# Small steps of a two-layer decoder trunk move between ScalarE, GpSimd and VectorE

## The chip, the cores and the metric

The kernel runs on one core of a Trainium2 chip. The metric is the time of one execution on the device in microseconds (us). The engines are called as the profile calls them: PE (TensorE, matmuls; PEld its weight loads), DVE (VectorE), ACT (ScalarE), POOL (GpSimd) and SP (SyncE, which issues the DMAs).

## The reference

One inference step of a trunk of two layers, for one prompt of 512 rows and 8 sample rows that share the weights (width 1024). Cut to what matters here:

```python
def causal_conv(x, buf, w, b):                 # both layers; 3072 channels, 4 taps
    xp = concatenate([buf, x], axis=1)
    out = b + sum(xp[:, i:i + L] * w[i] for i in range(4))
    return silu(out), xp[:, L:]                # the last 3 rows are an output

# layer 0: gated DeltaNet (8 heads) and GLA (4 heads) beside each other, then one output projection
# GLA, per head and chunk:   o = qe @ S + p @ v;   S = alast * S + kdec.T @ v
# per head:                  o2 = rmsnorm(o2, gla_norm_g) * silu(gate)
# layer 1: SSD, 32 heads in 4 groups; per head and chunk:
#                            y = elam * (c @ h) + m @ xdt;  h = last * h + xdec.T @ b
# per group:                 y = rmsnorm(y * silu(z), ssd_norm_g)
```

A sample has one new row and a state of its own, in the convolution (its last 3 rows, `buf`) as in the recurrences.

## The kernel before

The activations are held transposed, 128 channels on the partitions and 520 columns free: 512 of the prompt, cut in 4 chunks of 128, and 8 of the samples. A projection takes 128 columns of weights: `split_w` (L234) makes of them a rounded part on ACT (`w`, L248) and the rest by a subtraction on DVE, of every third or so on POOL; `project_half` (L258) runs 24 matmuls (L264 to L266, the last reads the rest) into one of two `pj` banks, or in layer 1 also `px`, first for columns 0 to 255, then for 256 to 519, whose last 8 are the samples.

`conv` (L431) takes the two halves: ACT copies them to SBUF (`xr`, L436), ACT scales `xr` by one tap (L437), POOL copies the last 11 columns (3 of the prompt, 8 of the samples) to `tail` (L438), DVE adds three taps, ACT takes the tanh (L442), DVE makes the SiLU of it. There are 48 such calls, 24 in each layer. `conv_samples` (L446) does the samples' convolution later, from `tail`, for 2 or 4 tiles at a time: two POOL operations, a tanh on ACT, one scaled product on DVE.

In layer 0, `gdn_samples` (L738) makes the samples' step of the DeltaNet per head, and `gla_head` (L837) a GLA head: per chunk PE makes `pd`, ACT scales it to `sn` (L892), DVE adds the old state; POOL scales the old state to `sp` (L886), which PE multiplies by the queries (L899); ACT squares the result for the norm (L902). After that come the samples: SP loads their states (L940), PE multiplies (L942), transposes (L955), sums squares over the partitions (L964), and the norm and gate are small operations on POOL and DVE. Beside this POOL runs the 62 steps of the triangular inverse (`sb` and `st` 64xN, from `gdn_blocks`, L618).

In layer 1, `ssd_group` (L1222) does a group of 8 heads: two convolutions for `b_` and `c_`, four for x. DVE makes decay matrices (`dec`), `kq` is a convolution's result, L1318 its transposes, L1345 and L1358 the products over chunks. `sample_x` (L1263) calls `conv_samples` and scales; `sample_state` (L1275) runs per pair of heads two POOL products with the state (`sb<-inv,st`), a sum on DVE, two POOL products for the update (`sb<-inv,smh`), 8 scalings on ACT and an addition on DVE. `sample_norm` (L1202) closes two groups.

A scheduler in the tile framework sets the order of the instructions on each engine, from the program's order, the buffers of each tile name (`BUFS`) and its own estimates of durations. So an edit in one place moves instructions elsewhere too. Each engine then runs its list in order, and waits where an input isn't there.

## Time and profile before

| | |
|---|---|
| median of 3 runs | 1144.23 us (1143.73 to 1147.21) |
| the profiled execution, its own time | 1146.9 us |
| its span, first to last instruction | 1145.1 us |
| granted TensorE clock, mean | 0.976 |
| PE busy | 1056.3 us, 92% |
| DVE busy | 763.1 us, 67% |
| ACT busy | 620.4 us, 54% |
| POOL busy | 576.5 us, 50% |
| DMA | 160 MB, 140 GB/s |

Of the span, layer 0 takes the first 650 us or so, layer 1 the rest. The shares are means over stages that differ: a stage is read by the stretch of the trace in which it lies. Names in the trace are those of the tiles; L141 is the helper for products and sums of two tiles, L144 that for a scaled product, so the tile says which step it is. The clock is given as a share of the full 2.4 GHz.

### The profile page before, as it was taken

The page shows a single profiled execution, that of the slowest core. Times are in us where ns is not written, and L with a number is a line of the kernel's source. Part 1 is how long each engine was busy: PE and PEld are TensorE (multiplying, and loading weights), DVE is VectorE, ACT ScalarE, POOL GpSimd, SP SyncE. Part 2 cuts the span into 40 slices and gives each one's busy share as a digit, 9 for nine tenths or more (in the row PEclk, how much of TensorE's full clock was granted, in tenths as well). Part 3 has the DMA queues.
Part 4 walks back from the last instruction along what each step waited for, and adds up shares of the span by engine and source line. Part 5 has one row for each costly group of instructions (what it writes and reads, how often), then busy time and mean ns, then how long its engine had stood idle before and what let it go on. Part 6 is the DMA issues. An engine that isn't in the chain of part 4 may idle for free.

```text
span 1145.1 us, 23024 instructions
## 1 busy us (share of the span) xinstructions
PE 1056.3 (92%) x8900; PEld 1006.4 (88%) x8900; DVE 763.1 (67%) x1265; ACT 620.4 (54%) x1458; POOL 576.5 (50%) x701
## 2 busy tenths in 40 slices
PE   8999989999999898999889989979988988988997
PEld 7999879899899897898889988869978978988997
DVE  5797354657776645656554468799889689766643
ACT  5566345544444644554333556855855765765452
POOL 4144962204143594226152534685497587468542
PEclk8999999999999999899997999999999999999999
DMA  5324245623544325544842434645755654656632
GB/s 162 90 80 110 68 146 157 190 56 107 166 135 117 114 79 165 180 133 136 246 126 71 131 97 132 190 131 149 218 148 149 187 165 132 208 174 194 185 89 76
DMA packets 241731, 160.00 MB, mean 140 GB/s; under 512 B 21463, under 2 KB 221358, under 8 KB 241606
## 3 DMA queue, kind: packets, MB, share of 16 engines
q1 hardware_dynamic: 241622, 158.53, 47.8%
q8 instruction: 70, 1.15, 0.4%
q14 instruction: 39, 0.32, 0.1%
HBM read 127.05 MB, written 31.84 MB: 139 GB/s over the span
## 4 chain that ended last, share of the span: by engine, by line
PE 40%; POOL 18%; DVE 17%; DMA 13%; issue 5%; ACT 4%; SPq 2%; DVEq 0%; POOLq 0%; ACTq 0%
PE pj L265 9%; PE pj L264 9%; PE pj L266 9%; POOL sb L141 8%; DVE f L144 4%; POOL st L141 3%; DVE w L141 2%; DMA sb<-ud 1%; DMA dec<-ldr 1%; PE px L265 1%; DVE st L141 1%; DVE kq L144 1%; PE px L264 1%; PE px L266 1%; DVE of L141 1%
## 5 line engine op out<-in xcount | busy, mean ns | idle before, releaser
L266 PE MATMUL pj<-ua,w 128*128 128x256 f32 x776 | 224.8, 290 | 5.3 <-DVE w L141 3.9
L264 PE MATMUL pj<-ub,w 128*128 128x264 f32 x768 | 225.6, 294 | 1.5 <-ACT ub L339 0.9
L264 PE MATMUL pj<-ua,w 128*128 128x256 f32 x776 | 224.5, 289 | 2.0 <-ACT vg L472 1.3
L266 PE MATMUL pj<-ub,w 128*128 128x264 f32 x768 | 224.4, 292 | 0.0
L265 PE MATMUL pj<-ub,w 128*128 128x264 f32 x742 | 218.3, 294 | 0.0
L265 PE MATMUL pj<-ua,w 128*128 128x256 f32 x750 | 217.0, 290 | 1.4 <-POOL ua L1028 1.4
L141 DVE TENSOR_TENSOR w<-raw,w 128x1024 fp32r<-128x1024 f32 x102 | 140.8, 1381 | 59.0 <-PE pj L265 30.1
L248 ACT ACTIVATE w<-raw 128x1024 fp32r<-128x1024 f32 x123 | 129.7, 1054 | 49.2 <-PE pj L266 10.6
L266 PEld LDWEIGHTS pj<-ua,w 128*128 128x128 f32 x776 | 149.6, 193 | 7.7 <-DVE w L141 4.3
L264 PEld LDWEIGHTS pj<-ua,w 128*128 128x128 f32 x776 | 149.4, 192 | 3.3 <-ACT vg L472 1.5
L264 PEld LDWEIGHTS pj<-ub,w 128*128 128x128 f32 x768 | 147.4, 192 | 3.1 <-ACT ub L339 1.1
L266 PEld LDWEIGHTS pj<-ub,w 128*128 128x128 f32 x768 | 147.1, 192 | 2.2 <-issue 2.0
L144 DVE SCALAR_TENSOR_TENSOR f<-xr,cvw,f 128x512 f32<-128x512 f32 x144 | 136.5, 948 | 17.5 <-ACT f L437 16.0
L265 PEld LDWEIGHTS pj<-ua,w 128*128 128x128 f32 x750 | 144.5, 193 | 3.7 <-issue 1.8
L265 PEld LDWEIGHTS pj<-ub,w 128*128 128x128 f32 x742 | 142.3, 192 | 2.0 <-issue 1.5
L438 POOL COPY tail<-xr 128x11 f32<-128x11 f32 x48 | 31.9, 666 | 86.7 <-ACT xr L436 70.4
L141 POOL TENSOR_TENSOR w<-raw,w 128x1024 fp32r<-128x1024 f32 x20 | 52.1, 2607 | 39.8 <-PE px L265 13.2
L141 POOL TENSOR_TENSOR sb<-inv,st 128x512 f32<-128x512 f32 x32 | 53.6, 1691 | 15.7 <-DMA inv<-bd 9.2
L442 ACT ACTIVATE f<-f 128x512 f32<-128x512 f32 x48 | 30.2, 628 | 56.8 <-DVE f L144 56.6
L1287 ACT ACTIVATE st<-st,c 128x128 f32<-128x128 f32 x128 | 41.2, 395 | 33.7 <-POOL sb L141 33.7
L436 ACT ACTIVATE xr<-pj 128x256 f32<-128x256 f32 (+1 forms) x72 | 27.4, 380 | 41.1 <-PE pj L266 40.8
L1340 ACT ACTIVATE dec<-dec,c 128x128 f32<-128x128 f32 x128 | 40.3, 390 | 10.3 <-DMA dec<-ldr 8.9
(564 smaller groups left out, 2825.3 us busy)
## 6 DMA issues: line engine op xcount, KB each, us to landing
raw<-in_e_w_in_dram SPq DMA_DIRECT2D x56, 512.0 KB
raw<-in_o_w_in_dram SPq DMA_DIRECT2D x40, 512.0 KB
out_dram<-st SPq DMA_DIRECT2D x32, 512.0 KB
raw<-in_e_w_out_dram SPq DMA_DIRECT2D x32, 256.0 KB
st<-in_state_ssd_dram SPq DMA_DIRECT2D x16, 512.0 KB
dec<-ldr SPq DMA_DIRECT2D x32, 256.0 KB
raw<-in_o_w_out_dram SPq DMA_DIRECT2D x32, 256.0 KB
sb<-vd SPq DMA_DIRECT2D x8, 512.0 KB
```

What stands on the lines that cost most here:

```text
L141: eng.tensor_tensor(out, a, b, op=op)
L144: dve.scalar_tensor_tensor(out, a, s, b, op0=op0, op1=op1)
L248: act.activation(wh, rv, AF.Copy)
L264: pe.matmul(ps, wh, uh[b], start=(k == 0), stop=False)
L265: pe.matmul(ps, wh, ul[b], start=False, stop=False)
L266: i0 = pe.matmul(ps, wl, uh[b], start=False, stop=(k == NK - 1))
L436: act.activation(hsl(xr[:, 3:3 + T], b), halves[b], AF.Copy)
L438: pool.tensor_copy(tail[:, :, j], xr[:, TP:TP + 11])
L442: act.activation(th, a, AF.Tanh)
L1287: act.activation(st[:, b], st[:, b], AF.Copy, scale=sc2[:, 1, pr, b:b + 1])
L1340: act.activation(rb[:, chunk(c)], rb[:, chunk(c)], AF.Relu, scale=-1.0, bias=lamc[:, c, h:h + 1])
```

## The change

Six edits, and new buffer counts (`s2` 3 in place of 2, `sp` 2 in place of 1):

1. `conv`: the last 11 columns go to `tail` by ACT, straight from the second half's PSUM bank (five calls of 48 that have no such bank read `xr`).
2. `conv_samples`: the scaled product on DVE becomes two POOL operations, th*a and +a.
3. `gdn_samples`: the last product and sum of each head go from DVE to POOL.
4. `gla_head`: `sp` is made by ACT with a column scale instead of by POOL.
5. End of `gla_head`: two POOL and two DVE operations per head become three POOL operations over both halves.
6. `sample_norm`: eight scaled products on DVE become two POOL operations.

```diff
@@ -111,7 +111,7 @@
 
     BUFS = {
         ...
-        "st": 2, "sb": 2, "smc": 6, "smp": 4, "sms": 9, "jk": 1, "c5": 4, "c2": 1, "jd": 1, "nss": 1, "nrs": 1, "ors": 3, "smt": 1, "s1": 3, "u1": 2, "s2": 2, "smh": 6, "sp": 1, "row": 2,
+        "st": 2, "sb": 2, "smc": 6, "smp": 4, "sms": 9, "jk": 1, "c5": 4, "c2": 1, "jd": 1, "nss": 1, "nrs": 1, "ors": 3, "smt": 1, "s1": 3, "u1": 2, "s2": 3, "smh": 6, "sp": 2, "row": 2,
     }
     PBUFS = {"pj": 2, "po": 2, "pr": 2, "px": 1, "ps": 1}
     uid = [0]
@@ -435,7 +435,7 @@
         for b in range(2) if halves else ():
             act.activation(hsl(xr[:, 3:3 + T], b), halves[b], AF.Copy)
         act.activation(a, xr[:, 3:3 + TP], AF.Identity, scale=cw[:, 72 + j:73 + j], bias=cw[:, 96 + j:97 + j])
-        pool.tensor_copy(tail[:, :, j], xr[:, TP:TP + 11])
+        act.activation(tail[:, :, j], halves[1][:, 253:264] if halves else xr[:, TP:TP + 11], AF.Copy)
         for i in range(3):
             stt(a, xr[:, i:i + TP], cw[:, i * 24 + j:i * 24 + j + 1], a, MULT, ADD)
         th = sb([P, TP], tag="f1")
@@ -450,7 +450,8 @@
         tt(pool, a, a, hp[:, js, :], ADD)
         th = sb([P, n, NS], tag="sms")
         act.activation(th, a, AF.Tanh)
-        stt(dst, th, 1.0, a, ADD, MULT)
+        tt(pool, th, th, a, MULT)
+        tt(pool, dst, th, a, ADD)
 
     def conv_states(tail, hist, out_p, out_s):
         dma(out_s[0, :, 0:2, :], hist[0, :, 1:3, :])
@@ -781,8 +782,8 @@
             tt(dve, uu, uu, sbeta[:, h, :], MULT)
             t2 = sb([P, NS], tag="sms")
             tt(dve, oo[:, j], pv[:, :, 1], eb, MULT)
-            tt(dve, t2, rk[:, 2, j], uu, MULT)
-            tt(dve, oo[:, j], oo[:, j], t2, ADD)
+            tt(pool, t2, rk[:, 2, j], uu, MULT)
+            tt(pool, oo[:, j], oo[:, j], t2, ADD)
             ps = bank("ps")
             pe.transpose(ps[0:NS, 0:P], uu, ident)
             ur = sb([NS, 256], tag="row")
@@ -883,7 +884,7 @@
             po = pos[-1][:, (c % 2) * 256:(c % 2) * 256 + 256]
             if c:
                 sp = sb([P, 256], tag="sp")
-                pool.tensor_scalar(sp, s_, em[:, c:c + 1], 0.0, op0=MULT, op1=ADD)
+                act.activation(sp, s_, AF.Copy, scale=em[:, c:c + 1])
             pd = bank("pr")
             for s in range(2):
                 es = slice(s * P, (s + 1) * P)
@@ -965,9 +966,9 @@
         rr = sb([P, NS], tag="sms")
         dve.tensor_scalar(rr, ps[:, 0:NS], 1.0 / 256.0, EPS, op0=MULT, op1=ADD)
         tt(pool, rr, rr, nhalf[:, 0:NS], POW)
-        for s in range(2):
-            tt(pool, os_[:, s, :], os_[:, s, :], rr, MULT)
-            stt(osm[:, 8 + 2 * h + s], os_[:, s, :], vec("glag", s, True), sg[:, 4 + s], MULT, MULT)
+        tt(pool, os_, os_, rr.unsqueeze(1).to_broadcast([P, 2, NS]), MULT)
+        tt(pool, os_, os_, sg[:, 4:6], MULT)
+        tt(pool, osm[:, 8 + 2 * h:10 + 2 * h], os_, bc3(vhalf[:, voff["glag"]:voff["glag"] + 2], NS), MULT)
 
     def gdn_pair(h0):
         heads = []
@@ -1212,10 +1213,9 @@
         rr = sb([P, 16], tag="sms")
         dve.tensor_scalar(rr, ps[:, 0:16], 0.25 / 512.0, EPS, op0=MULT, op1=ADD)
         tt(pool, rr, rr, nhalf[:, 0:16], POW)
-        for i in range(2):
-            for j in range(4):
-                pr = 4 * (g - 1 + i) + j
-                stt(ysm[:, pr], ysm[:, pr], vec("ssdg", pr, True), rr[:, i * NS:(i + 1) * NS], MULT, MULT)
+        tt(pool, yv, yv, rr.rearrange("p (g b) -> p g b", g=2).unsqueeze(2).to_broadcast([P, 2, 4, NS]), MULT)
+        v0 = voff["ssdg"] + 4 * g - 4
+        tt(pool, ysm[:, gs], ysm[:, gs], bc3(vhalf[:, v0:v0 + 8], NS), MULT)
 
     left = []
 
```

The edits shorten DVE's list by 58 instructions; ACT's grows by 60, 48 `tail` copies and 12 `sp`; POOL loses these 60 and gains as many small ones. The new order also moves other instructions. Line numbers of the changed kernel are one higher from `conv_samples` on. A number behind a name tells buffers and tiles apart.

First ACT's order in the third GLA head. `s_852` to `s_865` are the states of its four chunks, `sp` their scaled copies, `dec` the next head's decay (its exponential waits for DVE). Before:

```order
L892 ACTIVATE s_852_4915<-pr_4912,smc_4191 128x256
L902 ACTIVATE jk_4919,smc_4910<-po_4911 128x256
L892 ACTIVATE s_856_4926<-pr_4923,smc_4191 128x256
L845 ACTIVATE vg_5518<-pj_5525 128x256
L892 ACTIVATE s_861_4941<-pr_4938,smc_4191 128x256
L823 ACT_TABLE_LOAD
L823 ACTIVATE dec_5211<-dec_5212 128x512
L902 ACTIVATE jk_4933,smc_4910<-po_4911 128x256
L892 ACTIVATE s_865_4955<-pr_4952,smc_4191 128x256
L824 ACTIVATE dec_5212<-dec_5212 128x512
```

Now:

```order
L893 ACTIVATE s_852_4916<-pr_4913,smc_4192 128x256
L903 ACTIVATE jk_4920,smc_4911<-po_4912 128x256
L887 ACTIVATE sp_4922<-s_852_4916,smc_4190 128x256
L893 ACTIVATE s_856_4927<-pr_4924,smc_4192 128x256
L887 ACTIVATE sp_4937<-s_856_4927,smc_4190 128x256
L846 ACTIVATE vg_5518<-pj_5525 128x256
L893 ACTIVATE s_861_4942<-pr_4939,smc_4192 128x256
L903 ACTIVATE jk_4934,smc_4911<-po_4912 128x256
L824 ACT_TABLE_LOAD
L824 ACTIVATE dec_5211<-dec_5212 128x512
L893 ACTIVATE s_865_4956<-pr_4953,smc_4192 128x256
L887 ACTIVATE sp_4951<-s_861_4942,smc_4190 128x256
```

Two of the three `sp` stand right behind the state that they scale; the third (`sp_4951`, of `s_861`) stands behind the table load and the exponential.

Second PE's order in the same head's sample part: L955 (now L956) transposes its rows, L964 (L965) sums the squares over the partitions, the rest are projections (`pj`), the inverse (`px`) and a transpose of another head. Before:

```order
L955 MATMUL ps_5168<-ident,sb_5166 128x128 x4
L659 MATMUL px_5246<-inv_5243,inv_5226 32x32 x8
L684 MATMUL pr_6263<-ident,kq_3790 128x128 x4
L964 MATMUL ps_5179<-sms_5177,ones 128x8 x2
L264 MATMUL pj_6139<-ua_146,w_6135 128x256
L265 MATMUL pj_6139<-ua_148,w_6135 128x256
```

Now, from the transposes on, and then around the sum:

```order
L956 MATMUL ps_5169<-ident,sb_5167 128x128 x4
L264 MATMUL pj_6099<-ub_147,w_6070 128x264
L265 MATMUL pj_6099<-ub_149,w_6070 128x264
...
L265 MATMUL pj_6099<-ub_169,w_6070 128x264
L266 MATMUL pj_6099<-ub_167,w_6071 128x264
L264 MATMUL pj_6099<-ub_171,w_6070 128x264
L965 MATMUL ps_5180<-sms_5178,ones 128x8 x2
L265 MATMUL pj_6099<-ub_173,w_6070 128x264
```

Between the transposes and the sum there are now 19 matmuls of a projection, where there was none.

Third POOL's order in the first group of layer 1. `w` is a weight split's rest, `sb<-inv,st` and `sb<-inv,smh` are the products of `sample_state`, `c` and `smh` those of `sample_x`. Before:

```order
L141 TENSOR_TENSOR sb_9360<-inv_8861,smh_8875 128x512
L141 TENSOR_TENSOR sb_9360<-inv_8862,smh_8875 128x512
L141 TENSOR_TENSOR c_1588_8809<-sms_9175,sms_9184 128x16
L141 TENSOR_TENSOR w_9413<-raw_9410,w_9412 128x1024
L141 TENSOR_TENSOR sb_9554<-inv_8863,st_9552 128x512
L141 TENSOR_TENSOR sb_9554<-inv_8864,st_9552 128x512
L438 COPY tail_8808<-xr_320 128x11
L141 TENSOR_TENSOR sb_9558<-inv_8861,smh_8875 128x512
L141 TENSOR_TENSOR sb_9558<-inv_8862,smh_8875 128x512
L1310 COPY c_1589_8810<-vg_9168 128x8
```

Now:

```order
L141 TENSOR_TENSOR sb_9364<-inv_8864,smh_8878 128x512
L141 TENSOR_TENSOR sb_9364<-inv_8865,smh_8878 128x512
L141 TENSOR_TENSOR c_1588_8811<-sms_9178,sms_9188 128x16
L141 TENSOR_TENSOR sb_9559<-inv_8866,st_9557 128x512
L141 TENSOR_TENSOR sb_9559<-inv_8867,st_9557 128x512
L141 TENSOR_TENSOR sb_9563<-inv_8864,smh_8878 128x512
L141 TENSOR_TENSOR sb_9563<-inv_8865,smh_8878 128x512
L141 TENSOR_TENSOR w_9417<-raw_9414,w_9416 128x1024
L1310 COPY c_1589_8812<-vg_9171 128x8
```

The split (`w_9413`, now `w_9417`) stands behind four sample products instead of ahead of them, and the copy to `tail` is gone from among them. PE reads the split after about as many projection matmuls as before, and now has the transposes of L1318 right ahead of its first read of it.

## Rows read from the trace of the kernel before

**Rows 1.** The page's first two lines: span and number of instructions, and of each engine the busy time, its share of the span and its instructions.

```profile
span 1145.1 us, 23024 instructions
PE 1056.3 (92%) x8900; PEld 1006.4 (88%) x8900; DVE 763.1 (67%) x1265; ACT 620.4 (54%) x1458; POOL 576.5 (50%) x701
```

**Rows 2.** What PE waited for, over the whole span: engine, PSUM tile and line <- the engine, tile and line that released it: us in total, times, longest us.

```profile
PE pr L1318 <- DVE kq L144: 6.2, 7, 1.9
PE ps L942 <- DMA st<-in_state_gla_dram: 5.1, 3, 2.3
PE po L899 <- POOL sp L886: 4.0, 4, 1.9
PE px L266 <- POOL w L141: 3.4, 3, 1.8
PE ps L964 <- POOL sms L141: 2.0, 1, 2.0
```

**Rows 3.** Busy time of each engine in stretches of 25 us: start:end, length, us (x instructions) of PE, its weight loads, DVE, ACT and POOL, then the granted TensorE clock as a share of full speed, the DMA share and GB/s.

```profile
400.00:425.00 25.00, 23.07 (x186) 22.27 (x187) 14.43 (x20) 10.68 (x25) 23.45 (x36) 1.00 0.31 90
450.00:475.00 25.00, 21.11 (x198) 18.96 (x200) 12.85 (x27) 11.72 (x25) 5.81 (x11) 0.86 0.69 208
725.00:750.00 25.00, 21.77 (x184) 20.96 (x183) 23.24 (x21) 17.95 (x42) 20.21 (x16) 1.00 0.50 144
750.00:775.00 25.00, 19.14 (x159) 17.04 (x158) 23.20 (x22) 14.64 (x40) 21.40 (x23) 1.00 0.59 163
925.00:950.00 25.00, 19.76 (x162) 18.24 (x161) 22.86 (x20) 15.65 (x44) 21.64 (x20) 1.00 0.50 141
```

**Rows 4.** POOL's groups of instructions, each shape apart: line, operation, out<-in, shapes, count | busy us, mean ns of one | idle time before them and what ended it.

```profile
L438 POOL COPY tail<-xr 128x11 f32<-128x11 f32 x48 | 31.9, 666 | 86.7 <-ACT xr L436 70.4 <-ACT xr L362 13.3 <-ACT xr L488 2.9
L886 POOL TENSOR_SCALAR sp<-s,smc 128x256 f32<-128x256 f32 x12 | 7.0, 582 | 7.6 <-PE po L899 6.0 <-ACT s L892 1.5
L141 POOL TENSOR_TENSOR sms<-sms,hp 128x16 f32<-128x16 f32 x12 | 4.8, 402 | 0.7
L141 POOL TENSOR_TENSOR sms<-smh,c 128x32 f32<-128x32 f32 x4 | 3.5, 870 | 0.0
```

**Rows 5.** The same view, ACT's groups: the copy with a column scale, and a small copy out of PSUM.

```profile
L947 ACT ACTIVATE st<-st,smc 128x256 f32<-128x256 f32 x32 | 13.4, 496 | 10.3 <-PE ps L942 10.3
L935 ACT ACTIVATE sms<-ps 128x8 f32<-128x8 f32 x4 | 0.7, 176 | 1.5 <-PE ps L933 1.5
```

**Rows 6.** The view of one tile, `tail`, the row of its copy: count: duration ns min/median/max, first and last start, shape.

```profile
L438 POOL COPY tail<-xr x48: 204/671/1213, 34.1 to 1015.7; 128x11 f32<-128x11 f32 x48
```

**Rows 7.** PE's timeline around seven instructions: start us, duration us, engine, line, operation, out<-in, tile, count, and in brackets the idle time before it and what ended it. The matmuls of one projection go by threes; between 736.43 and 738.58 there are 18.

```profile
400.43 0.49 PE L899 MATMUL po<-sp,kqg 128*128 128x128 f32 x2 [1.90 <-POOL sp L886]
...
452.31 0.64 PE L942 MATMUL ps<-st,sms 128*32 128x256 f32 x8 [1.92 <-DMA st<-in_state_gla_dram]
...
461.42 1.02 PE L964 MATMUL ps<-sms,ones 128*128 128x8 f32 x4 [1.98 <-POOL sms L141]
...
735.98 0.39 PE L266 MATMUL px<-ua,w 128*128 128x256 f32 x1 [1.83 <-POOL w L141]
...
736.43 0.28 PE L266 MATMUL px<-ua,w 128*128 128x256 f32 x1
...
738.58 0.28 PE L266 MATMUL px<-ua,w 128*128 128x256 f32 x1
...
933.73 0.38 PE L266 MATMUL pj<-ua,w 128*128 128x256 f32 x1 [3.16 <-DVE w L141]
```

**Rows 8.** ACT's timeline in the third GLA head, same columns.

```profile
400.41 0.47 ACT L892 ACTIVATE s<-pr,smc 128x256 f32<-128x256 f32 x1 [3.67 <-POOL sp L886]
...
404.63 0.63 ACT L823 ACTIVATE dec<-dec 128x512 f32<-128x512 f32 x1 [2.44 <-DVE dec L141]
```

**Rows 9.** DVE's groups, each shape apart: two of the small steps of the samples.

```profile
L144 DVE SCALAR_TENSOR_TENSOR sms<-sms,sms 128x16 f32<-128x16 f32 x12 | 2.3, 192 | 0.7 <-ACT sms L452 0.7
L144 DVE SCALAR_TENSOR_TENSOR c<-c,vhalf,sms 128x8 f32<-128x8 f32 x16 | 2.4, 220 | 0.3 <-POOL sms L141 0.3
```

**Rows 10.** POOL's timeline in the first group of layer 1.

```profile
732.59 3.34 POOL L141 TENSOR_TENSOR w<-raw,w 128x1024 fp32r<-128x1024 f32 x1
735.88 3.97 POOL L141 TENSOR_TENSOR sb<-inv,st 128x512 f32<-128x512 f32 x2
...
740.41 2.95 POOL L141 TENSOR_TENSOR sb<-inv,smh 128x512 f32<-128x512 f32 x2
```

**Rows 11.** DVE's timeline in the same place.

```profile
728.39 0.69 DVE L141 TENSOR_TENSOR dec<-dec,kqg 128x512 f32<-128x512 f32 x1
...
733.62 2.85 DVE L141 TENSOR_TENSOR dec<-dec,kqg 128x512 f32<-128x512 f32 x1
```

**Rows 12.** What PE waited for between 740 and 775 us, columns as in the second group.

```profile
PE po L1345 <- DVE ch L141: 2.6, 2, 1.6
PE pr L1358 <- POOL ap L141: 1.8, 1, 1.8
PE pr L1318 <- DVE kq L144: 1.3, 2, 1.0
PE pj L266 <- DVE w L141: 0.8, 1, 0.8
PE po L1345 <- ACT ch L1325: 0.7, 1, 0.7
```

## The prediction

> **What bounds the kernel now.** First the page's head [rows 1]: PE is busy 1056.3 of 1145.1 us, so all of PE's idle time is 88.8 us, and no edit that leaves the matmuls alone can win more. Then the table of PE's waits [rows 2], which tells who holds PE up: no single cause is large. Of those that the change touches, the prompt's GLA product with `sp` waits 4.0 us for POOL in four places, the sample norm's sum (L964) 2.0 us for POOL once, a `px` projection 3.4 us in three places for POOL's share of a weight split. Then the stretches of 25 us [rows 3]: two kinds of place are to be seen. In layer 0 at 400 to 425 us POOL is full (23.45) while DVE has 10 us to spare; in layer 1 at 725 to 775 and 925 to 950 us DVE is full (22.9 to 23.2), POOL nearly (20.2 to 21.6), and PE falls to 19 to 22. There a microsecond on DVE or POOL can be one of the program. So the change is summed in two parts, by layer.
>
> The sum is made against the profiled execution, 1146.9 us (span 1145.1 plus 1.8 around it). The median of the runs is 1144.23, 2.7 us lower; I take the same 2.7 off the result. Faster or slower means by over 0.3%, 3.4 us, about what a measurement of this kernel can tell.
>
> **`sp` to ACT (layer 0).** POOL does 12 of them, 0.582 us each, 7.0 us [rows 4]. ACT has the same form with a column scale, 128x256 at 0.496 us [rows 5], so ACT gets 12 x 0.5 = 6 us, where it is busy 10.7 of 25. What counts is the wait: PE stood 1.90 us at 400.43 [rows 7] for an `sp` that sat in POOL's queue between pieces of the inverse, and ACT stood 3.67 us at 400.41 [rows 8] for the buffer that POOL still read. On ACT, `sp` stands right behind the `s` that it scales, so POOL's queue leaves the chain: 4.0 us of waits go [rows 2]. What is late next: in the third head ACT now has the `sp` of the last chunk behind the table load and the exponential that stood 2.44 us for DVE at 404.63 [rows 8], and PE's product with it now comes earlier among the projections. That gives back 0 to 2.44 us; I take 1.5, since DVE's scan there isn't sped up by the change. Sum −2.5; bounds −4.0 (nothing comes back) and +2 (half of the 4.0 goes, and in each of four heads two `sp` of 0.5 us hold up what stands behind them on ACT).
>
> **End of `gla_head`, sample steps of GDN (layer 0).** At the end of `gla_head` eight scaled products, two a head, leave DVE and POOL gets one operation more a head; in `gdn_samples` 16 small operations go from DVE to POOL. Neither sits ahead of a wait of PE in [rows 2], and DVE has room; the time is 0, covered by DVE's 10 free microseconds in 25, and some 16 x 0.4 = 6.4 us of POOL time [rows 4] would have to fit if POOL were the bound. The one wait there, L964 for POOL at 461.42, 1.98 us [rows 7], goes for another reason: the order now puts 19 projection matmuls between the transposes and it. A matmul takes 0.12 us (18 from 736.43 to 738.58 [rows 7]), so 2.3 us of work lie over a wait of 1.98. Sum −2.0; bounds −2.0 and 0 (the samples' chain is later by as much).
>
> **Sample loads of GLA.** PE waits 5.1 us in three places for the state from DMA [rows 2], 1.92 of it at 452.31 [rows 7]. SP issues these loads in nearly the old order; PE's products come some 19 matmuls earlier among the projections, their heads finish earlier too. I take 0, between −2.7 (the last two waits gone) and +2.4 (19 x 0.12, the load no earlier).
>
> **Tail copies to ACT.** POOL loses 48 x 0.666 = 31.9 us [rows 4]. ACT gets 48 copies of 11 columns, 43 of them out of PSUM; the trace has none, the nearest is 128x8 from PSUM at 0.176 [rows 5], so some 8.4 us in all, half of it in layer 1. They stand between the second `xr` copy and the weight copy or the scaled `xr` that starts DVE's taps: each convolution starts 0.18 us later. In layer 1 that is 24 x 0.18 = 4.3 us at most, if DVE has nothing else, and 0 if it has, as [rows 3] says for most of it. I take +0.5; bounds 0 and +4.3.
> How much POOL really gets back is to be weighed. The tile view [rows 6] has the copy at 0.204 us at best, 0.671 in the middle, 1.213 at worst: its own work is 0.2, the rest is standing. The other side shows in layer 1: a DVE product of 0.69 us at 728.39 takes 2.85 at 733.62 and ends 0.54 us after POOL's 3.34 us split of 732.59 has ended [rows 10, 11]. The Trainium skill, "SBUF — State Buffer", section "Who interferes with whom", says that a DVE instruction with two SBUF inputs and a POOL instruction that reads SBUF exclude each other, and that the one that comes second fully blocks; these rows agree. By it a tail copy frees 0.2 us, not 0.67, every small step put on POOL costs DVE a little again, and the next term would be 0 in place of −1.5: 1142.2 in all.
>
> **Steps off DVE (layer 1).** The scaled product after the samples' tanh goes, 12 times 0.192 us; the 16 of `sample_norm` go, 2.4 us busy in all [rows 9]: 4.7 us off DVE. POOL gets 24 small products at 0.40 and four wider ones at up to 0.87 [rows 4], 13 us, about what 24 tail copies gave it. `sample_norm` lies at the ends of groups, off the full stretches, so I count a third, −1.5; bounds −4.7 and 0.
>
> **POOL's weight split in the first group (layer 1).** The order has moved it: before it stood ahead of four sample products, now behind them. They took 3.97 and 2.95 us [rows 10], so 6.9 us, while PE comes to the split after the same number of projections and already stood 1.83 us for it at 735.98 [rows 7]. So the wait there grows by up to 6.9. Against that, from 740 to 775 us PE stood another 7.2 us [rows 12], nearly all for DVE, which is full: what PE loses early it doesn't wait again, as long as DVE has other taps to run. Some 30% stays, since of those 7.2 us 2.6 hang on POOL or on a weight split, which the delay may lengthen: +2; bounds 0 and +6.9.
>
> **Sum**: −2.5 −2.0 +0 +0.5 −1.5 +2.0 = −3.5: 1143.4 in the profiled execution, **1140.7 us** against the median.
>
> **The rivals.**
> *A, DVE paces layer 1 throughout*: each of its 4.7 us counts and the late split is absorbed whole: −2.5 −2.0 +0.5 −4.7 = −8.7, 1135.5. For it: 22.9 to 23.2 of 25 [rows 3]. Against: `sample_norm` isn't in those stretches.
> *B, slower: PE stands for the late split and its clock falls.* The place is the `px` projection of 735.98. If the wait grows to 1.8 + 6.9 = 8.7 us and nothing absorbs it, the sum loses its absorbed 4.9 and the DVE term's 1.5: −3.5 + 6.4 = +2.9. At 450 to 475, after stalls at 452 and 461, the granted clock was 0.86 [rows 3], that is 7 of 25 us at the lower level (1.2 GHz), 3.5 us lost; after the 3.16 us stall of 933.73 [rows 7] it stayed 1.00 [rows 3]. [...] Then +6.4: 1150.6. Against: PE now also has its transposes (L1318) in that place, which must wait for DVE anyway.
> *C, no change: a swap.* What leaves DVE comes back as standing for POOL (the 1.5), and the 2.5 of `sp` is waited again where the next load or scan sets the time: −3.5 + 4.0 = +0.5, 1144.7. The rows of 733.62 and 452.31 speak for it. The Trainium skill, "Perfetto Trace Analysis", section "Optimizing Scalar/DVE Operations", says that work moved between those two engines might not help as they share a read port: that is this rival. What speaks against is that the `sp` waits were for POOL's queue, not for a port.
>
> **Numbers.** Forecast 0.42, A 0.18, B 0.18, C 0.22. The forecast lies at the edge, 3.5 against 3.4 us, so half of it counts as faster: 0.42 x 0.57 + 0.18 = 0.42. Same takes the rest of it and most of C: 0.38; slower B and a little of C: 0.20. The range goes from 1134, a little under A, to 1150, nearly B; all low bounds together (−13.4) or all high ones (+15.6) would need six mishaps of one sign; some 15% lie outside. The likeliest case alone has 1138 to 1143.
>
> **What would show it.** Right: no PE wait for `sp` from POOL, none at L964; the tail copy on ACT near 0.18; POOL some 10 us less busy, DVE too (58 operations of 0.16 to 0.23 us); a longer wait of PE at the split near 735 us, and shorter ones for DVE behind it. Wrong: a granted clock under 1.00 near 735 to 750 (B); DVE products stretched as often as before with the stretch from 725 to 775 as long as it was (C); a new wait of PE for ACT's `sp` of several us in the third head; tail copies well over 0.2 us.

## The result and the profile after

The changed kernel is slower: 1149.03 us median of 20 runs against 1142.62 of 20 runs before, ratio 1.0050, 95% interval 1.0029 to 1.0071, so 6.4 us by the medians. The profiled execution took 1149.07 us (span 1147.3, mean granted clock 0.974). The profiled one of before, 1146.9, lay 4 us above the median of its later runs: a difference of a few us between two profiles is no result here, and the ratios decide. Three slow executions further down, one each of e3, e11 and e15 (3444.50, 1153.40 and 1245.86 us), count in the medians of their rows and not in the ratios.

The page's head of the changed kernel, to be read against [rows 1]:

```profile
span 1147.3 us, 23004 instructions
PE 1055.2 (92%) x8900; PEld 1007.9 (88%) x8900; DVE 757.4 (66%) x1207; ACT 628.0 (55%) x1518; POOL 563.8 (49%) x701
```

The work moved as announced: DVE has 58 instructions and 5.7 us less, POOL 12.7 us less, ACT 7.6 us more. PE's busy time is the same within 1.1 us, so the loss is in how its work is strung together. ACT's groups show the prices that the forecast had to guess, 0.190 us for a copy of 11 columns out of PSUM and 0.504 for `sp`:

```profile
L438 ACT ACTIVATE tail<-pj 128x11 f32<-128x11 f32 x36 | 6.9, 190 | 0.0
...
L887 ACT ACTIVATE sp<-s,smc 128x256 f32<-128x256 f32 x12 | 6.0, 504 | 5.6 <-DVE s L144 5.6
...
L438 ACT ACTIVATE tail<-xr 128x11 f32<-128x11 f32 x5 | 1.0, 215 | 0.0
```

What PE waited for in the changed kernel (us in total, times, longest), against [rows 2]:

```profile
PE pr L1318 <- DVE kq L144: 11.4, 6, 4.7
PE ps L943 <- DMA st<-in_state_gla_dram: 6.3, 3, 3.5
...
PE px L653 <- DVE inv L644: 3.6, 1, 3.6
...
PE po L898 <- ACT jk L903: 2.8, 1, 2.8
```

The 4.0 us for POOL's `sp` and the 2.0 us at the sample norm's sum are gone. For `sp` PE now stands 1.6 us, once, and waits for ACT. Longer waits have come elsewhere: 3.5 us in one piece for a sample load, 3.6 for the inverse, 2.8 for a square on ACT, and 4.7 in one piece at the transposes of L1318. PE's timeline at these five places, against [rows 7] (start, duration, in brackets the idle time before and its releaser):

```profile
396.05 0.49 PE L900 MATMUL po<-sp,kqg 128*128 128x128 f32 x2 [1.61 <-ACT sp L887]
...
403.44 0.49 PE L898 MATMUL po<-ch,ch 128*128 128x128 f32 x2 [2.85 <-ACT jk L903]
...
439.58 1.08 PE L943 MATMUL ps<-st,sms 128*32 128x256 f32 x8 [3.52 <-DMA st<-in_state_gla_dram]
...
473.31 0.64 PE L653 MATMUL px<-inv,ap 32*32 32x32 f32 x16 [3.64 <-DVE inv L644]
...
733.83 1.12 PE L1318 MATMUL pr<-ident,kq 128*128 128x128 f32 x4 [4.73 <-DVE kq L144]
```

DVE's and POOL's timelines before that last stall, against [rows 10] and [rows 11]:

```profile
728.52 1.22 DVE L1282 TENSOR_REDUCE smh<-sb 128x8 f32<-128x1024 f32 x1 [1.19 <-POOL sb L141]
729.65 1.37 DVE L141 TENSOR_TENSOR dec<-dec,kqg 128x512 f32<-128x512 f32 x1
730.95 2.83 DVE L144 SCALAR_TENSOR_TENSOR kq<-f,f 128x512 f32<-128x512 f32 x1
```

```profile
724.51 3.98 POOL L141 TENSOR_TENSOR sb<-inv,st 128x512 f32<-128x512 f32 x2
728.45 2.04 POOL L141 TENSOR_TENSOR sb<-inv,smh 128x512 f32<-128x512 f32 x2
730.44 2.79 POOL L141 TENSOR_TENSOR w<-raw,w 128x1024 fp32r<-128x1024 f32 x1
```

The four sample products have passed the split, as the order showed. DVE's sum over them stands ahead of `kq` in DVE's list and waits 1.19 us for POOL; then `kq` runs beside POOL's split and takes 2.83 us, where the middle one of its 40 like takes 0.687, as the view of the tile `kq` has it (ns, min/median/max):

```profile
L144 DVE SCALAR_TENSOR_TENSOR kq<-f,f x40: 660/687/2826, 41.9 to 1025.1; 128x512 f32<-128x512 f32 x40
```

So the late split is not what PE stands for: by then it is done, and PE stands for `kq`, which its transposes, ahead of the `px` matmuls, read.

Busy time and granted clock in 5 us stretches there (columns as in [rows 3]), and five of PE's matmuls behind the stall:

```profile
725.00:730.00 5.00, 4.10 (x35) 3.90 (x33) 3.81 (x4) 5.00 (x15) 5.00 (x4) 1.00 0.61 185
730.00:735.00 5.00, 1.17 (x6) 1.17 (x7) 4.40 (x4) 1.99 (x4) 3.42 (x3) 0.77 0.46 123
735.00:740.00 5.00, 5.00 (x34) 4.71 (x33) 5.00 (x5) 0.57 (x2) 4.24 (x3) 0.55 0.38 103
```

```profile
734.96 0.41 PE L264 MATMUL px<-ua,w 128*128 128x256 f32 x1
735.17 0.41 PE L265 MATMUL px<-ua,w 128*128 128x256 f32 x1
735.39 0.41 PE L266 MATMUL px<-ua,w 128*128 128x256 f32 x1
...
738.16 0.41 PE L264 MATMUL px<-ua,w 128*128 128x256 f32 x1
738.37 0.41 PE L265 MATMUL px<-ua,w 128*128 128x256 f32 x1
```

Behind a stretch in which PE was busy 1.17 of 5 us the clock is 0.55, nearly all at its lower level, and matmuls start 0.21 us apart in place of 0.12 [rows 7]: the 16 steps from 734.96 to 738.37 cost 1.5 us more. The same stretch of 25 us has a clock of 0.86, before 1.00 [rows 3].

### The profile page after: what moved, and what is told of

It is laid out like the page before. It is cut to its first block, busy times and chain, and to the rows that moved or that the text cites. A ratio compares the mean times of both kernels' runs of the same rounds, so it can differ in the third digit from the quotient of the medians.

```text
span 1147.3 us, 23004 instructions
## 1 busy us (share of the span) xinstructions
PE 1055.2 (92%) x8900; PEld 1007.9 (88%) x8900; DVE 757.4 (66%) x1207; ACT 628.0 (55%) x1518; POOL 563.8 (49%) x701
## 4 chain that ended last, share of the span: by engine, by line
PE 37%; POOL 20%; DMA 15%; DVE 15%; ACT 5%; issue 5%; SPq 2%; DVEq 0%; POOLq 0%; ACTq 0%
POOL sb L141 9%; PE pj L264 8%; PE pj L266 8%; PE pj L265 8%; POOL st L141 3%; DVE f L144 3%; DVE w L141 2%; DMA sb<-ud 2%; POOL sms L141 1%; DMA dec<-ldr 1%; DMA pre<-ldr 1%; ACT dec L1340 1%; DMA inv<-bd 1%; DVE kq L144 1%; POOL ap L141 1%
## 5 line engine op out<-in xcount | busy, mean ns | idle before, releaser
L266 PEld LDWEIGHTS pj<-ua,w 128*128 128x128 f32 x776 | 151.6, 195 | 6.8 <-DVE w L141 3.0
L264 PEld LDWEIGHTS pj<-ua,w 128*128 128x128 f32 x776 | 151.7, 195 | 3.4 <-issue 1.4
L265 PEld LDWEIGHTS pj<-ua,w 128*128 128x128 f32 x750 | 146.4, 195 | 2.1 <-POOL ua L1029 1.3
L144 DVE SCALAR_TENSOR_TENSOR f<-xr,cvw,f 128x512 f32<-128x512 f32 x144 | 132.4, 920 | 15.0 <-ACT f L437 13.5
L141 POOL TENSOR_TENSOR sms<-sms,sms 128x16 f32<-128x16 f32 (+2 forms) x56 | 25.1, 450 | 81.6 <-ACT sms L957 44.1
L141 POOL TENSOR_TENSOR sb<-inv,st 128x512 f32<-128x512 f32 x32 | 56.5, 1782 | 14.2 <-DMA inv<-bd 8.9
```

Source lines behind the costliest of these rows:

```text
L141: eng.tensor_tensor(out, a, b, op=op)
L144: dve.scalar_tensor_tensor(out, a, s, b, op0=op0, op1=op1)
L264: pe.matmul(ps, wh, uh[b], start=(k == 0), stop=False)
L265: pe.matmul(ps, wh, ul[b], start=False, stop=False)
L266: i0 = pe.matmul(ps, wl, uh[b], start=False, stop=(k == NK - 1))
```

## Experiments

All runs went against the kernel before on the same chip, in five rounds on five chips (e1 to e4, e5 to e8, e9 to e12, e13 to e16, e17 and e18); each row has 12 runs, e9 and e12 six. Where an expectation names a theory by a letter (others are explained where they are named): **Q**, `sp` costs through ACT's queue, which stands at the decay's exponential (Q2: through ACT's time in general); **R**, what PE no longer waits for `sp` is waited again elsewhere, in the order that comes with it, whoever makes `sp`; **T**, each `tail` copy on ACT delays its convolution; **O**, the copies cost through the new order in layer 1's first group; **L**, every other order of this kernel is slower.

| run | what is in it | median us | ratio to before, 95% interval |
|---|---|---|---|
| e1 | edit 1 | 1146.15 | 1.0046 (1.0021 to 1.0070) |
| e2 | edits 2 to 6 | 1145.69 | 1.0032 (1.0010 to 1.0054) |
| e3 | edit 4 and buffers | 1148.18 | 1.0049 (1.0029 to 1.0069) |
| e4 | all, POOL's split first | 1145.61 | 1.0026 (1.0001 to 1.0051) |
| e5 | e3, exponential behind the squares | 1150.23 | 1.0049 (1.0018 to 1.0080) |
| e6 | all, with both constraints | 1147.00 | 1.0025 (0.9999 to 1.0051) |
| e7 | edits 3, 5 | 1139.73 | 0.9972 (0.9940 to 1.0003) |
| e8 | edits 2, 6 | 1143.38 | 1.0010 (0.9985 to 1.0034) |
| e9 | the buffer counts alone | 1150.76 | 1.0088 (1.0064 to 1.0112) |
| e10 | e3, `sp` by DVE | 1148.49 | 1.0063 (1.0039 to 1.0088) |
| e11 | edit 1 in layer 0 | 1140.42 | 0.9998 (0.9975 to 1.0021) |
| e12 | edit 1, copies behind the scaled `xr` | 1152.14 | 1.0090 (1.0068 to 1.0112) |
| e13 | edit 1 in group 1 of layer 1 | 1144.13 | 1.0017 (0.9993 to 1.0041) |
| e14 | edit 1 in groups 2 to 4 | 1141.65 | 0.9990 (0.9964 to 1.0015) |
| e15 | edits 3, 5, and 1 in layer 0 | 1141.91 | 0.9982 (0.9961 to 1.0003) |
| e16 | edit 4, and 1 in layer 0 | 1144.48 | 1.0019 (0.9995 to 1.0044) |
| e17 | all but edit 4 | 1146.37 | 1.0027 (0.9999 to 1.0055) |
| e18 | e17, group 1's copies on POOL | 1139.59 | 0.9967 (0.9942 to 0.9993) |

### The change in parts (e1, e2, e3, e7, e8)

Each run has the lines of the named edits, as in the diff above, and the others as before; e3 also has the buffer counts (`sp` 2, `s2` 3).

> The kernel before with edit 1 alone (tail copies on ACT). Its order of POOL and PE in the first group of layer 1 is that of the changed kernel: the weight split behind four sample products, the transposes L1318 ahead of the px projection. Theory O (that order is what costs: PE stands 4.7 us for kq there and its clock falls behind it): 4 to 6 us slower than before, with a wait of PE over 3 us at L1318 near 735 us. Theory T (each of the 48 copies makes its convolution 0.19 us later): also 4 us slower, but spread over layer 1 and with no long wait in that place. Theory S (the small sample steps on POOL cost): no change or faster by 1 to 2 us, since POOL only loses work.

> The changed kernel without edit 1 (tail copies stay on POOL). In the first group of layer 1 the transposes L1318 stand where they stood before. Theories O and T: 1 to 3 us faster than before (the sp waits of 4.0 us are gone, what edits 2 and 6 do is small). Theory S: as slow as the changed kernel, 5 us over before.

> The kernel before with edit 4 alone (sp on ACT); the order of layer 1 is that of before, instruction by instruction on PE. If the term of my sum is right: 2.5 us faster, from 4.0 to +2. If sp on ACT only puts the wait elsewhere (rival): within 1 us of before, with new waits of PE for ACT or DMA of 3 us or more between 395 and 450 us.

> The kernel before with edits 3 and 5 alone (the last product and sum of gdn_samples, the end of gla_head, from DVE to POOL). PE's order is that of before but for one place. My term: 0, within 1.5 us of before. Rival L: 3 to 4 us slower than before. Rival P (small steps on POOL delay the inverse and the samples): 2 us slower, with longer waits of PE for POOL or DVE between 450 and 480 us.

> The kernel before with edits 2 and 6 alone (the samples' SiLU and the sample norm of layer 1 on POOL). PE's transposes L1318 in the first group stay where they were, others move by up to 31 matmuls. My term: 1.5 us faster, from 4.7 to 0. Theory O says no stall over 3 us comes. Rival L or P: 3 to 4 us slower than before.

Two edits lose on their own: edit 1 by 0.46%, edit 4 with its buffer counts by 0.49%, some 5 us each. So the forecast of e3, 2.5 us faster, missed, and so did that of e2, 1 to 3 us faster: it holds edit 4 too. Edits 3 and 5 may bring 0.28% (their interval reaches 1.0003), 2 and 6 nothing that shows. PE's stalls in e1 and e3, first of all, are those that the changed kernel has:

```profile
729.99 1.12 PE L1318 MATMUL pr<-ident,kq 128*128 128x128 f32 x4 [4.73 <-DVE kq L144]
```

```profile
164.84 1.08 PE L942 MATMUL ps<-st,sms 128*32 128x256 f32 x8 [3.80 <-DMA st<-in_state_gla_dram]
...
412.25 0.51 PE L897 MATMUL po<-ch,ch 128*128 128x128 f32 x2 [4.81 <-ACT jk L902]
```

### The split first; the exponential behind the squares (e4, e5, e6)

e4 is the changed kernel with the second pair's products held behind POOL's split in the first group; e5 is e3 with the next head's exponential held behind the last square; e6 is the changed kernel with both.

```diff
-            for q in range(2):
-                tt(pool, tmp[:, 4 * q:4 * q + 4], bcb[1][q], st[:, 4 * q:4 * q + 4], MULT)
+            with ExitStack() as first:
+                if (g, j) == (0, 1):
+                    first.enter_context(tc.issue_after(lastsplit[0]))
+                for q in range(2):
+                    tt(pool, tmp[:, 4 * q:4 * q + 4], bcb[1][q], st[:, 4 * q:4 * q + 4], MULT)
...
-        act.activation(e1[:, 0:TP], e2[:, 0:TP], AF.Exp)
+        with ExitStack() as behind:
+            if lastsq:
+                behind.enter_context(tc.issue_after(lastsq[0]))
+            act.activation(e1[:, 0:TP], e2[:, 0:TP], AF.Exp)
```

> The changed kernel with one constraint: in the first group of layer 1 the sample products of the second pair of heads are issued behind the weight split on POOL, as in the kernel before. DVE's kq then stands ahead of the sum over these products; the transposes L1318 stay ahead of the px projection on PE. Theory O: 3 to 5 us faster than the changed kernel (so 1 to 3 us over before), with PE's wait at L1318 under 3 us and the granted clock near 1.00 behind it. Theory T or S: the same time as the changed kernel within 1 us, about 6 us over before.

> Edit 4 alone (sp on ACT), and the two exponentials of the next head's decay are issued on ACT behind the last square of the running GLA head; PE's order is that of edit 4 alone. Theory Q (in the third head sp and the squares stand on ACT behind an exponential that waits for DVE; PE then stands 4.8 us in one piece and its clock falls): the wait of 4.8 us near 412 us is gone, 1 to 2 us faster than before, 5 to 7 faster than edit 4 alone (1148). Rival N (sp on ACT costs by itself, by ACT's time): still 4 us or more over before, the wait at 412 gone or not. Rival L (any other order than the one before is some 4 us slower, this one was the best of many): also still 3 us or more over before.

> The changed kernel with both constraints: the exponentials behind the running GLA head's last square, and in the first group of layer 1 the second pair's sample products behind the weight split on POOL. Theories Q and O together: neither the stall near 403 us (2.9 for the square) nor that of 4.7 at L1318; 1140 to 1143 us, not slower than before, 6 to 9 faster than the changed kernel. Rival L: 1145 to 1147 as the other variants.

The constraint of e4 takes the stall near 730 from 4.73 to 2.77 us, and its ratio is 1.0026 against the changed kernel's 1.0050; the intervals overlap. A new stall of 3.96 us for POOL stands at 765. e6, with both constraints, was forecast at 1140 to 1143 us and missed it: 1147.00, a ratio of 1.0025. e3's wait at 412 looked like Q: ACT's timeline shows the square behind a table load that stood 5.74 us for DVE.

```profile
403.30 0.38 ACT L902 ACTIVATE jk<-po 128x256 bf16<-128x256 f32 x1
...
409.51 1.28 ACT L823 ACT_TABLE_LOAD   x1 [5.74 <-DVE dec L141]
410.81 0.63 ACT L823 ACTIVATE dec<-dec 128x512 f32<-128x512 f32 x1
411.35 0.49 ACT L886 ACTIVATE sp<-s,smc 128x256 f32<-128x256 f32 x1
411.74 0.36 ACT L902 ACTIVATE jk<-po 128x256 bf16<-128x256 f32 x1
```

With the exponential behind the square (e5) the kernel is as slow, PE still waits 4.02 us for `jk` at 410.48, and 4.02 for the sample load at 163.03. But the square now stands behind `sp`, which waits for DVE's sum of the state, and that stands behind the next head's scan:

```profile
405.20 2.65 DVE L151 TENSOR_TENSOR_SCAN dec<-ones,dec 128x128 f32<-128x128 f32 x4
...
409.56 0.51 ACT L890 ACTIVATE sp<-s,smc 128x256 f32<-128x256 f32 x1 [6.41 <-DVE s L144]
409.97 0.36 ACT L906 ACTIVATE jk<-po 128x256 bf16<-128x256 f32 x1
```

So e5 moved the stall instead of taking it away: the exponential is not all that the square stands behind, and whether ACT's queue costs is left to the next runs.

### Who makes `sp`, and the buffers alone (e9, e10, e16)

e9 has the buffer counts of edit 4 and nothing else; e10 has them too (its expectation says one buffer) and `dve.tensor_scalar` in place of `pool.tensor_scalar`; e16 is edit 4 with the `tail` copies of layer 0 on ACT.

```diff
-                pool.tensor_scalar(sp, s_, em[:, c:c + 1], 0.0, op0=MULT, op1=ADD)
+                dve.tensor_scalar(sp, s_, em[:, c:c + 1], 0.0, op0=MULT, op1=ADD)
```

> The kernel before with edit 4's buffer counts alone (sp 2, s2 3); sp stays on POOL. PE's order of the transposes is that of before. Theory Q2 (the cost of edit 4, 5 us, is that sp stands in ACT's queue): this takes the waits for the one sp buffer away without ACT work, 0 to 2 us faster than before. Rival B2 (the buffers are the cost: the states live longer, or the order of loads changes): 3 us or more slower than before.

> The kernel before with sp made by DVE in place of POOL (one buffer, as before); PE's transposes stand as with edit 4 alone. Theory Q2 (ACT's queue): DVE has room there, no wait of PE for a square of 4 us; within 2 us of before, 3 us or more under edit 4 alone (1148). Rival R (what costs is PE's new order in the third GLA head and what follows it, whichever engine makes sp): 4 us or more over before, as edit 4 alone.

> Edit 4 with edit 1 in layer 0 alone: ACT makes sp, and the DeltaNet's transposes of the first heads stand where they stood before, not 20 and 16 matmuls earlier as with edit 4 alone. Theory R (edit 4 costs by the order that comes with it): the stretch from the first sample product of the DeltaNet to the next column sums takes 85 to 88 us and not 91, and the whole 2 to 4 us less than edit 4 alone, 0 to 3 over before. Theory N (sp's work or place on ACT costs): as slow as edit 4 alone, 5 over before.

`sp` on DVE loses as much as on ACT, and without ACT's stall: in e10 PE waits once for `sp` from DVE and 1.0 us for `jk`, where e3 waited 4.81, and most for the samples' states:

```profile
PE ps L942 <- DMA st<-in_state_gla_dram: 7.8, 2, 4.0
...
PE po L899 <- DVE sp L886: 2.3, 1, 2.3
...
PE po L897 <- ACT jk L902: 1.0, 1, 1.0
```

So Q and Q2 fall. The buffer counts alone, `sp` still on POOL, lose 0.88%, more than edit 4 with them: rival B2 of e9's expectation. The order in layer 0 is another one there too, and PE's waits for POOL's `sp` are not gone, against [rows 2]:

```profile
PE po L899 <- POOL sp L886: 4.2, 3, 1.9
```

So that loss needs neither another engine for `sp` nor a wait that moves on. No run has `sp` on ACT with the old counts: the counts, the order that comes with them and the engine aren't told apart. Where the loss lies is read from PE's timeline by milestones of layer 0's first half: first product of the first GLA head (`po<-ch,ch`), its first sample product (`ps<-st,sms`), the inverse's next step (`px<-inv,ap`), the first DeltaNet sample product (`ps<-st,c`), and not the next column sums (`px<-ones,pre`), which come 26 to 29 us on, but the ones after those. Us between them, one profile each:

| | to sample product | to inverse | to DeltaNet sample | to column sums | sum |
|---|---|---|---|---|---|
| before | 38.7 | 7.0 | 93.3 | 87.8 | 226.8 |
| e3 (ACT) | 36.0 | 9.7 | 95.7 | 90.8 | 232.2 |
| e5 (ACT, exponential later) | 36.2 | 9.5 | 97.6 | 91.0 | 234.3 |
| e10 (DVE) | 36.1 | 10.0 | 95.9 | 90.9 | 232.9 |
| e9 (POOL, buffer counts alone) | 37.8 | 6.6 | 99.0 | 86.5 | 229.9 |
| e16 (ACT, with edit 1 in layer 0) | 35.8 | 8.7 | 95.8 | 85.3 | 225.6 |
| the changed kernel | 35.6 | 8.7 | 95.8 | 85.6 | 225.7 |

e13 and e14, which have the instructions and the order of before in layer 0, have sums of 224.7 and 225.5: a difference of 2 us is nothing here. The sums hold nearly the same work (1974 to 1985 matmuls), the columns don't: in e3's first column PE has 179 projection matmuls and not 198, 2.3 us less at 0.12 us each, and 14 of them come in the second, where PE waits for nothing. So the 2.7 us of the first column are work put off, not the gain that was forecast. At the end of the first column PE waits longer for the sample's load, in e3 3.80 us (its line stands with e1's above), before 2.34:

```profile
167.94 1.08 PE L942 MATMUL ps<-st,sms 128*32 128x256 f32 x8 [2.34 <-DMA st<-in_state_gla_dram]
```

Over all four e3, e5 and e10 lose 5 to 10 us, whoever makes `sp`, and e9 some 4. With edit 1 in layer 0 (e16) the last column is 85 us and the sum as before; the time is 1.0019 against e3's 1.0049, as R forecast, though the intervals overlap. e11, edit 1 in layer 0 alone, also has 85.0 there, and no change in time that shows. So edit 4's loss hangs on the order around it, and in the changed kernel this stretch takes no longer than before.

### The `tail` copies (e11 to e14)

e13, the six copies of layer 1's first group on ACT; e14 has `> 0` in the condition (groups 2 to 4, 18 copies), e11 `if cw is cvw[0]` (layer 0, 24 copies):

```diff
-        pool.tensor_copy(tail[:, :, j], xr[:, TP:TP + 11])
+        if cw is cvw[1] and (j % 4 if j > 15 else j // 4) == 0:
+            act.activation(tail[:, :, j], halves[1][:, 253:264] if halves else xr[:, TP:TP + 11], AF.Copy)
+        else:
+            pool.tensor_copy(tail[:, :, j], xr[:, TP:TP + 11])
```

e12 has all 48 on ACT, each held behind the scaled `xr` of its convolution, so that DVE's taps wait for none.

> Edit 1 in layer 0 alone (24 tail copies on ACT); in layer 1 they stay on POOL and PE's order there is that of before. Theory O (edit 1 costs by the order in layer 1): within 1.5 us of before. Theory T (each copy makes its convolution later, DVE's chain or not): 2 us slower, half of edit 1 alone.

> Edit 1 alone, but each tail copy is issued on ACT behind the scaled xr that starts DVE's taps, so the taps are not 0.19 us later; the bank of the second half is held 0.8 us longer. PE's order in the first group of layer 1 still has the transposes L1318 early (60 matmuls). Theory T: the time of before within 1 us. Theory O: 4 us or more over before, as edit 1 alone, with a wait over 3 us at L1318 near 730 us.

> Edit 1 for the six convolutions of the first group of layer 1 alone. The order there is that of the changed kernel (transposes L1318 34 matmuls earlier, weight split behind four sample products), everywhere else that of before. Theory O (one place's order, with PE's 4.7 us stall and the clock behind it): 3 to 5 us slower than before. Theory T (each copy costs by itself): 6 of 24 copies, about 1 us.

> Edit 1 for the eighteen convolutions of groups two to four of layer 1 alone; the first group's order is that of before, groups three and four have PE's transposes moved by up to 30 matmuls. Theory O: within 1.5 us of before. Theory T: 18 of 24 copies, 3 to 4 us slower.

24 copies in layer 0 and 18 in groups 2 to 4 cost nothing that shows, each set by itself; T's 2 us for the first would still lie inside e11's interval, its 3 to 4 us for the second lie outside e14's. Taking the copy off the convolution's path (e12) made it worse, not better, with 1.97 us at L1318 near 739 in place of the stall that O forecast; why e12 loses 0.90% stays open. T falls by e12 and e14. Six copies in group 1 reproduce the stall to the hundredth, with the releaser:

```profile
730.24 1.12 PE L1321 MATMUL pr<-ident,kq 128*128 128x128 f32 x4 [4.73 <-DVE kq L144]
```

but alone they cost 0.17% (−0.07 to 0.41), under the 3 to 5 us that O forecast and about a third of e1's 0.46%. So the stall that is largest in the table can't be laid down as the whole loss; the intervals overlap.

### Taking the two losing pieces out (e15, e17, e18)

e15 keeps the parts that hadn't lost by then; it was forecast 2 to 4 us faster and has 0.9982 with an interval that reaches 1.0003. e17 is the changed kernel with edit 4 undone; e18 is e17 with the six copies of group 1 back on POOL:

```diff
-            act.activation(tail[:, :, j], halves[1][:, 253:264] if halves else xr[:, TP:TP + 11], AF.Copy)
+            if not (cw is cvw[1] and (j % 4 if j > 15 else j // 4) == 0):
+                act.activation(tail[:, :, j], halves[1][:, 253:264] if halves else xr[:, TP:TP + 11], AF.Copy)
+            else:
+                pool.tensor_copy(tail[:, :, j], xr[:, TP:TP + 11])
```

> Edits 3 and 5, and edit 1 in layer 0 alone: the parts that cost nothing each by itself. If they add up: 2 to 4 us faster than before. If their order in layer 0 (some transposes of the fourth GLA head 58 and 81 matmuls earlier) makes a new stall: 2 us or more slower.

> The changed kernel with edit 4 and its buffers undone (sp on POOL, sp 1, s2 2). By sums of the edits alone (R and O): edit 1 costs about 5 us, the ends and the DeltaNet samples give back about 3, small steps of layer 1 cost about 1, so +2 to +3 against before: 1144 to 1146, a ratio of 1.001 to 1.003; no wait of PE for jk in the third GLA head, and the stall of over 4 us at the L1318 transposes near 730 is there. If edit 4 were not the main cost (the edits only disturb each other): as the whole change, 1.005 or more. If edit 4 is all there is: 1.000 or less.

> The same, and POOL keeps the six tail copies of group 1 of layer 1. By O: the stall of over 4 us at L1318 near 730 is gone and 1 to 3 us less than the kernel beside it: 1141 to 1143, a ratio of 0.998 to 1.001. If edit 1 costs by the other groups together: the same time as the kernel beside it (within 1 us). By rival L (each other order is slower): 1.003 or more.

e17 is at 1.0027, as the sum of the parts said; its stall near 730 is 3.26 us, not over 4. e18 is at 0.9967, faster than before by 0.33% (0.07 to 0.58) and the one version of eighteen whose interval lies under 1, so that its lead over before is weak by itself. Between the two, on the same chip, six copies of 0.19 us make 6.0 us by the means of 12 runs each (4.0 to 8.0); in layer 0 the two have the same instructions in the same order on PE, DVE, ACT and POOL. L falls with e7, e11 and e14, which are not slower, and with e18. And e18 has a stall as long at the same place, the one that the forecast feared:

```profile
732.51 0.58 PE L266 MATMUL px<-ua,w 128*128 128x256 f32 x1 [4.40 <-POOL w L141]
```

Where the 6 us lie is read from PE's progress in layer 1: us from the second norm's first matmul until a share of the 3561 matmuls recorded from there on has started, one profile each. Nine profiles (before, e3, e5, e7, e9, e10, e11, e15, e16) have the same instructions in the same order there, on PE, DVE, ACT and POOL; their range is what one order gives.

| | 1/4 | 1/2 | 3/4 | all |
|---|---|---|---|---|
| before | 125.2 | 242.3 | 362.9 | 478.7 |
| the nine with the order of before | 125.0 to 128.5 | 242.3 to 246.0 | 362.1 to 368.5 | 478.1 to 484.4 |
| the changed kernel | 127.2 | 246.8 | 372.5 | 488.1 |
| e17 (the changed kernel's order) | 126.7 | 246.2 | 369.9 | 486.1 |
| e18 | 124.7 | 243.2 | 364.4 | 480.4 |

At a quarter, past the stall of 4.73 us and its low clock, the changed kernel lies inside the range; before stood there too, in more pieces [rows 12]. Behind it the changed kernel and e17 leave the range, by some 5 us against its mean of 481.6, in the groups that follow, where no single wait stands out; e18 doesn't. The other profiles agree: the seven kernels with group 1's copies on ACT (the changed one, e1, e4, e6, e12, e13, e17) take 484.2 to 490.3 us for layer 1, 486.8 in the mean, the thirteen without 478.0 to 484.5, 481.5 in the mean. So O is right in that group 1's copies decide, and wrong in where: the stall alone doesn't carry it. That it comes by the order of what follows is what is left, not shown: which instruction decides stays open.

## Why the prediction was wrong

The forecast was 1140.7 with 1134 to 1150 around it; 1149.03 lies inside, on the wrong side of no change. Two terms of the sum failed, that of `sp` and that of the `tail` copies, and one is missing, for the buffer counts.

**`sp` to ACT, −2.5.** ACT's price was right (0.504 against 0.5), and PE no longer waits for POOL's `sp`. What failed is the term for what comes back: 1.5 was taken of the 4.0, and the changed kernel has 1.61 us for ACT's `sp` at 396.05 and 2.85 at 403.44 for a square behind the exponential that was named as late next, 4.5 in all by the same counting. Alone, with its buffer counts, the edit costs 5.6 us (3.3 to 7.9, from e3), beyond the bound of +2. That half of rival C, "waited again where the next load or scan sets the time", fits what e3 and e5 show, the load (3.80 us against 2.34) and the sum behind the scan (6.41 us), but was priced too low. The buffer counts have no term in the sum at all, and alone they cost 0.88% (e9); how much of edit 4's loss is theirs stays open. Inside the whole change the step weighs less: e17, without it, is at 1.0027 against 1.0050, and e16 stands at 1.0019 against e11's 0.9998, both differences inside the intervals.

**`tail` copies, +0.5, bound +4.3.** Price right (0.190 against 0.18), mechanism wrong. It was priced as a delay of each convolution; 42 of the 48 copies cost nothing that shows (e11, e14), six cost 6.0 us in e18's company and some 2 alone. The step failed in costing an instruction by its duration where it sets the order of a group.

**POOL's split, +2, and rival B.** The split came late, PE stalled near 734 and the clock fell to 0.55 behind it, as B said; PE stood for `kq`, not for the split. The 7.2 us of waits between 740 and 775 were not "nearly all for DVE": by [rows 12] 4.7 are. That PE doesn't wait again what it lost early was right all the same: in the changed kernel PE has, behind the stall and up to 775, two waits left, 1.6 us in all.

```profile
PE pr L1358 <- POOL ap L141: 0.9, 1, 0.9
PE pr L1318 <- DVE kq L144: 0.7, 1, 0.7
```

B's time, 1150.6, is near the result by luck: it comes from a wait of 8.7 us that nothing absorbs, and the stall of 4.73 leaves nothing clear at the quarter mark. The length of one stall didn't tell the clock either: before, 0.86 stood behind two of 1.92 and 1.98 us, 1.00 behind one of 3.16 [rows 3, 7]. And the fallen clock (1.5 us) doesn't decide the kernel: e18 stalls 4.40 at this place, with a clock of 0.59 there, and wins.

```profile
730.00:735.00 5.00, 2.49 (x11) 2.49 (x12) 4.81 (x4) 2.44 (x9) 5.00 (x4) 0.59 0.54 150
```

**DVE's product beside POOL.** `kq` took 2.83 us beside POOL's split of 2.79, against 0.687 in the middle. By the Trainium skill, "SBUF — State Buffer", section "Who interferes with whom", a DVE instruction with two inputs in SBUF and a POOL instruction that reads SBUF exclude each other, and the second is blocked by the first; this row agrees. So the step that weighed it against POOL's relief was right to count little: DVE's 58 instructions less brought 5.7 us of busy time, and the 34 of edits 2 and 6 no time that shows (e8: 1.0010).

**L964 and the ends, −2.0.** The wait is gone, as forecast, but that it was worth 2.0 us isn't shown: e11 has lost it too and is at 0.9998, in e13 and e14, with the order of before in layer 0, it is 0.6 us, and e7, at −0.28% (−0.60 to +0.03), still has it:

```profile
PE ps L964 <- POOL sms L141: 1.8, 1, 1.8
```

**The sum.** By layers: for layer 1 it had +1.0, and the changed order takes some 5 us more there. For layer 0 it had −4.5; up to the second norm the changed kernel took 652.2 us, and three profiles of the order of before (before, e13, e14) took 659.4, 648.5 and 650.4, so that a gain of this size can be neither seen nor denied. By the ratios of parts: edit 1 +0.46, edit 4 +0.49, edits 3 and 5 −0.28, 2 and 6 +0.10, together +0.77% where +0.50 (0.29 to 0.71) was measured: near, but each part has an interval of 0.2 to 0.3 to either side, and the parts disturb each other (e16, e18). The clock goes with it in part: the changed kernel's 20 runs have a mean granted clock of 0.971, the 35 runs of before beside e1 0.979. But e14 has 0.975 against 0.979 at the same time, so how much of the 6.4 us the clock makes is not shown.

## What to carry to other kernels

Where a scheduler sets the order, an edit's price isn't its instruction's duration: six copies of 0.19 us were worth 6 us, two buffer counts 0.9%. So price the order: ask what PE reaches sooner and who is then late, give every changed buffer count a term of its own, and run each edit alone and left out. The longest wait in the table need not be the loss: two kernels 6 us apart had one of 3.3 and of 4.4 us in the same place, the faster kernel the longer. And before two profiles are compared, look at how far profiles of one and the same order lie apart: here up to 6 us in layer 1 and 11 in layer 0.

## What the runs showed of the hardware

A copy of 128x11 on ACT takes 0.190 us out of PSUM and 0.215 out of SBUF; the same copy on POOL had 0.67 in the middle [rows 6]. Behind a stall of 4.73 us, at a granted clock of 0.55, matmuls started 0.21 us apart in place of 0.12, which cost another 1.5 us.
